# NSA and MoBA trunk on one core: chains of x by token tile and halves, the compression sum beside a query chunk, gate 1 summed in the first attention, half accumulators at the outputs

## The chip, the cores and the metric

The kernel runs on one core of a Trainium2 chip. The time is that of the whole execution on the device in microseconds. Three runs are timed; the profile is of one further execution.

## The reference

A trunk of two layers over x (256 tokens, width 1024). In each layer a normalised x is scaled and shifted by vectors made from c, goes through an attention mixer, and is added back times a gate. Layer 0 is an NSA mixer (16 query heads, 4 key heads of width 64; a compressed, a selected and a window branch, mixed by sigmoid gates; compression flattens 15 blocks of 32 tokens, stride 16, to 2048 and sends them through two matmuls), layer 1 a MoBA mixer (256 tokens are one block, so it is plain causal attention).

```python
cond = jax.nn.silu(c)
for i in range(DEPTH):
    shift, scale, gate = jnp.split(cond @ ada_w[i] + ada_b[i], 3, axis=-1)
    h = rms_norm(x, norm_g[i]) * (1 + scale[:, None, :]) + shift[:, None, :]
...
    x = x + gate[:, None, :] * y
...
q, kc, vc, ks, vs, kw, vw, gl, z = split_cols(h @ w_in, [Q_W] + [KV_W] * 6 + [3 * N_HEADS, Q_W])
...
    return jax.nn.gelu(flat @ cmp_w1[i] + cmp_b1[i]) @ cmp_w2[i]
...
    return gc[..., 0:1] * o_cmp + gc[..., 1:2] * o_slc + gc[..., 2:3] * o_win
...
return (o * jax.nn.silu(z)) @ w_out
```

## The kernel before

Every instruction is first recorded in a plan (class `Plan`) and then issued by its greedy list scheduler, so nearly every row of the profile has the line of that issue loop, L361, and rows are told apart by their tiles. Each recorded operation has a level: FIRST_OF_ALL (-2), URGENT (-1), CHAIN (0) or FILL (1); on each engine the ready operation with the lowest level goes first, by the planner's own cost estimates. Tiles come from tags with a few buffers each (`hi`, `lo`: 4, `raw`: 5, `early`: 12, `ps`: 6 and `acc`: 2 banks of PSUM); a `ps` bank is 512 columns.

Matmuls in full precision are made of three: each fp32 weight is split by `parts_of` into `hi` (cast by ScalarE) and `lo` (the rest, subtracted by VectorE), and `product` adds hi times hi, hi times lo and lo times hi. HT holds the transposed, normalised and scaled h in the same two parts; its scale and shift per column are the small tile AB.

In order of the work: (1) x is loaded, squared and scaled by its rstd (`rstd_of`, eight small VectorE steps from `ss` to `rs`), transposed into xT, and by `affine` and `h_parts` made into HT, one or two of its eight column tiles at a time, as the vectors shift and scale arrive. Those come from `ada_rows`: matmuls of `early` weights (1024 by 128 or 256) with condz, the silu of c, in four column groups of 32 rows (shift and scale, two groups each), a `row` copy, and the selP matmul that turns a row to columns. `SPINS` matmuls on the identity come before. (2) The k and v products, for each of four row groups kp and four column groups ci, in the order of the table START, with `ada_rows` between. (3) `make_k` norms and ropes the keys; the tables for rope and norm (`tables`, on GpSimd) come from positions and small vectors that SyncE loads in `small_loads`. FLAT holds the blocks for compression, p<-ps,RT in the rows. (4) `chunk` makes queries 0 to 255 and the branch gates in 304 columns, then the compression's first sum `hid` (acc<-raw,p in the rows), the gelu, then the next query chunk; with spread, `chunk` calls `beside` after each weight, which moves one step of the generators in the list `side`: gate 0, shift and scale of layer 1. (5) z by `z_blocks`, the first half at once, the second one step per pair. (6) Eight `pair_a` of the first attention, each with one `beside`. (7) `out_products` with 512-column accumulators per token tile m and half ch; after the last product of each, `x_half` updates X and squares it and `next_h` makes layer 1's HT. (8) Layer 1 likewise; gate 1 is summed by VectorE in `ada_gate(1)`, eight operations of 128 by 1024 spread over the query chunks, then a matmul with ones, and two additions onto a bias that a DMA has broadcast. (9) z, eight `pair_b`, the last `out_products`, and for each accumulator y = acc times gate, X + y, and the output's DMA.

## Time and profile before

| | us |
|---|---|
| median of three runs | 330.7 (329.78 to 332.0) |
| profiled execution | 330.94 |
| its span, first to last instruction | 329.2 |
| TensorE, VectorE, ScalarE busy | 314.0, 239.5, 196.0 |

The three runs are whole executions; the span leaves out 1.7 us before the first and after the last instruction. Busy time says how long an engine had an instruction in work; what counts for the time is where TensorE, which is busy 95% of the span, has nothing in work, and for whom it waits.

### The profile page before, as it was taken

How to read it: one execution, taken by the hardware profiler on the slowest of the kernel's cores; microseconds unless marked ns; L12 is line 12 of the kernel's file. 1: busy time of each engine (PE TensorE's matmuls, PEld its weight loads, DVE VectorE, ACT ScalarE, POOL GpSimd, SP SyncE). 2: the span in 40 equal slices, each digit the busy share in tenths (PEclk: the TensorE clock that was granted, in tenths of full speed). 3: DMA queues.
4: the chain of work that ended last, by engine and by line, in shares of the span. 5: the costliest groups of instructions: out<-in, count | busy, mean ns of one | idle time of the engine just before them, and what ended most of it. 6: DMA issues, size and time to landing. Idle time of an engine off the chain costs nothing.

```text
span 329.2 us, 5934 instructions
## 1 busy us (share of the span) xinstructions
PE 314.0 (95%) x2135; PEld 249.9 (76%) x2135; DVE 239.5 (73%) x569; ACT 196.0 (60%) x467; POOL 25.7 (8%) x97
## 2 busy tenths in 40 slices
PE   5899999999899999999999999989999989999994
PEld 4666676897668669867878878767777989888883
DVE  1643473789999869623788867699999999984663
ACT  4534153664796463553797973786467699884420
POOL 6000896000000000000000000000000000000000
PEclk9999999999999999999999999999999999999999
DMA  7989999545948698849337138237988450303002
GB/s 246 336 251 370 364 357 319 161 145 183 344 172 319 214 326 290 257 137 326 117 120 265 64 89 280 79 113 241 315 304 286 157 186 3 127 0 100 29 34 96
DMA packets 43876, 66.83 MB, mean 203 GB/s; under 512 B 3800, under 2 KB 20295, under 8 KB 43847
## 3 DMA queue, kind: packets, MB, share of 16 engines
q1 hardware_dynamic: 43678, 66.40, 60.7%
q8 instruction: 17, 0.28, 0.3%
q14 instruction: 13, 0.10, 0.1%
q10 hardware_dynamic: 168, 0.06, 0.1%
HBM read 65.40 MB, written 1.05 MB: 202 GB/s over the span
## 4 chain that ended last, share of the span: by engine, by line
PE 80%; DVE 8%; DMA 6%; ACT 3%; issue 1%; ACTq 0%; SPq 0%
PE ps L361 44%; PE acc L361 36%; DMA early<-in_nsa_w_in_dram 3%; DMA raw<-in_nsa_w_out_dram 2%; DMA y<-in_nsa_cmp_b_dram 2%; DVE rs L361 1%; ACT hi L361 1%; DVE n_out L361 1%; DVE lo L361 1%; DVE y L361 1%; DVE tiny L361 1%; ACT p L361 1%; DVE X L361 1%; DVE KTA L361 1%; ACTq L361 0%
## 5 line engine op out<-in xcount | busy, mean ns | idle before, releaser
L361 DVE TENSOR_TENSOR lo<-raw,hi 128x1024 fp32r<-128x1024 f32 (+1 forms) x50 | 59.2, 1186 | 12.6 <-ACT hi L361 12.1
L361 ACT CAST hi<-raw 128x1024 fp32r<-128x1024 f32 (+1 forms) x50 | 51.0, 1027 | 28.4 <-PE acc L361 11.6
L361 PE MATMUL acc<-hi,HT 128*128 128x512 f32 (+1 forms) x176 | 57.8, 392 | 0.1
L361 PE MATMUL acc<-HT,hi 128*128 128x256 f32 x256 | 49.0, 286 | 1.0 <-DVE zT L361 1.0
L361 ACT ACTIVATE p<-ps,tiny 128x128 f32<-128x128 f32 (+1 forms) x96 | 39.7, 436 | 4.8 <-DVE tiny L361 4.6
L361 PEld LDWEIGHTS acc<-HT,hi 128*128 128x128 f32 x256 | 40.0, 189 | 2.4 <-DVE zT L361 2.1
L361 PEld LDWEIGHTS acc<-hi,HT 128*128 128x128 f32 x176 | 32.2, 188 | 8.5 <-issue 1.1
L361 PE MATMUL acc<-HT,lo 128*128 128x256 f32 x128 | 36.5, 286 | 0.0
L361 PE MATMUL acc<-lo,HT 128*128 128x512 f32 (+1 forms) x88 | 34.0, 387 | 0.0
L361 PE MATMUL ps<-KTA,qg 128*128 128x256 f32 (+1 forms) x192 | 30.7, 297 | 0.0
L361 PE MATMUL ps<-hi,HT 128*128 128x512 f32 (+1 forms) x96 | 28.0, 364 | 0.0
L361 PEld LDWEIGHTS ps<-KTA,qg 128*128 128x128 f32 x192 | 26.2, 191 | 2.2 <-issue 1.5
L361 DVE TENSOR_REDUCE tiny<-ps 128x2 f32<-128x512 f32 (+2 forms) x40 | 24.8, 630 | 2.7 <-PE ps L361 2.4
L361 ACT COPY pT<-ps 128x384 f32<-128x384 f32 x48 | 21.2, 498 | 6.2 <-PE ps L361 6.2
L361 PEld LDWEIGHTS acc<-HT,lo 128*128 128x128 f32 x128 | 24.1, 189 | 0.3 <-issue 0.2
L361 PE MATMUL ps<-hi,qg 128*128 128x512 f32 x64 | 22.2, 395 | 0.0
L361 PE MATMUL acc<-hi,qg 128*128 128x512 f32 x64 | 22.0, 394 | 0.0
L361 ACT ACTIVATION_READ_ACCUMULATOR p<-ps,tiny 128x1 f32 x96 | 21.2, 221 | 0.0
L361 PE MATMUL ps<-identF,p 128*128 128x128 f32 x144 | 20.5, 275 | 0.4 <-ACT p L361 0.4
L361 PEld LDWEIGHTS ps<-hi,HT 128*128 128x128 f32 x96 | 17.1, 189 | 3.6 <-issue 1.2
L361 PEld LDWEIGHTS acc<-lo,HT 128*128 128x128 f32 x88 | 16.6, 188 | 3.3 <-issue 0.5
L361 PE MATMUL ps<-pT,VA 128*64 128x256 f32 (+1 forms) x192 | 18.7, 333 | 0.0
(194 smaller groups left out, 560.1 us busy)
## 6 DMA issues: line engine op xcount, KB each, us to landing
raw<-in_ada_w_dram SPq DMA_DIRECT2D x32, 512.0 KB, 4.3
raw<-in_moba_w_in_dram SPq DMA_DIRECT2D x20, 512.0 KB, 5.1
early<-in_ada_w_dram SPq DMA_DIRECT2D x16, 512.0 KB, 9.9
early<-in_nsa_w_in_dram SPq DMA_DIRECT2D x12, 512.0 KB, 8.7
raw<-in_nsa_w_in_dram SPq DMA_DIRECT2D x12, 512.0 KB, 4.3
raw<-in_nsa_cmp_w_dram SPq DMA_DIRECT2D x8, 512.0 KB, 4.4
raw<-in_nsa_w_out_dram SPq DMA_DIRECT2D x8, 512.0 KB, 3.7
raw<-in_moba_w_out_dram SPq DMA_DIRECT2D x8, 512.0 KB, 4.7
```

Source lines behind the costliest of these rows:

```text
L361: r = getattr(self.engines[e], method)(*[self._real(a) for a in args], **{k: self._real(a) for k, a in kw.items()})
```

## The change

- Start: the sum of squares, rstd and scaling are separate for the two token tiles, and the scaling goes by halves of 512 columns, half on VectorE and half on ScalarE. The transposed small vectors (`columns(R, 8)`) come behind them. The first two `ada_rows` (128 columns) are made in two halves of two column groups each, with the row copied by VectorE. AB is one operation less. `affine` writes HT's high part from ScalarE and VectorE makes the low part. The first weights are split by k. The small loads come one by one behind the weights of later kp, the tables after the eighth entry of START. The planner counts a DMA of short rows at 1.4 times its bytes. Spins use X, so they wait for its load.
- Compression's sum becomes `cmp_steps`, a generator in `side`, one step per weight of the first query chunk.
- Gate 0 and gate 1 take the bias as one row (of g, or of the gate tile, which GpSimd clears) instead of a broadcast to 128 rows and an addition; ScalarE copies the result. The eight operations of gate 1 all are multiply-adds, and stand in `side`, which `pair_a` moves on by three steps each (one for the last two).
- z's first half goes with `beside` steps; the second query chunk and MoBA's are without spread.
- `out_products` has two accumulators of 256 columns in place of the last 512 for token tile 0 in the first output and for tile 1 in the second; X's update, squares and output DMA go by these slices.

```diff
+    smalls = small_loads()
...
-                with plan.at(level), plan.group():
-                    for k in range(kk - run + 1, kk + 1):
-                        for s in range(2):
-                            j = s * 2 + k % 2
-                            T.matmul(acc[32 * j:32 * j + 32, :n], condz[:, k, :], w[s][:, k % step, :],
+                for half in ((0,), (1,)) if n == P else ((0, 1),):
+                    with plan.at(level), plan.group():
+                        for k in range(kk - run + 1, kk + 1):
+                            for s in half:
+                                j = s * 2 + k % 2
+                                T.matmul(acc[32 * j:32 * j + 32, :n], condz[:, k, :], w[s][:, k % step, :],
...
-        A.copy(g, acc[:, :n])
+        if n == P:
+            V.tensor_copy(g, acc[:, :n])
+        else:
+            A.copy(g, acc[:, :n])
...
-        Q.dma_start(gate, row_to_all(ada_b, l * 3 * D + 2 * D, D))
+        bias = bass.AP(tensor=ada_b.tensor, offset=ada_b.offset + l * 3 * D + 2 * D, ap=[[D, 1], [1, D]])
         if l:
-            acc = tile_of("gate", D)
+            G.memset(gate, 0.0)
+            Q.dma_start(gate[0:1], bias)
             for kk in range(8):
                 w = ada_piece(l, kk, 2 * D, D)[:, 0, :]
                 with plan.at(FILL):
-                    if kk:
-                        V.scalar_tensor_tensor(acc, w, condz[:, kk, 0:1], acc, op0=OP.mult, op1=OP.add)
-                    else:
-                        V.tensor_scalar_mul(acc, w, condz[:, kk, 0:1])
+                    V.scalar_tensor_tensor(gate, w, condz[:, kk, 0:1], gate, op0=OP.mult, op1=OP.add)
                 yield
...
-            V.tensor_add(gate[:, sl], t, gate[:, sl])
+                T.matmul(t, mix[s], src[s], start=True, stop=True)
+                A.copy(gate[:, s * 512:(s + 1) * 512], t)
...
-    columns(R, 8)
-    ss = tile_of("ss", 16)[:, 0:2]
+        ss = [tile_of("ss", 16)[:, 0:1] for m in range(2)]
...
-        r = rstd_of(ss, 2, 1.0 / D)
-        V.tensor_scalar_mul(xs[0], X[:, 0, :], r[:, 0:1])
-        A.activation(xs[1], X[:, 1, :], AF.Copy, scale=r[:, 1:2])
+        r = [rstd_of(ss[m], 1, 1.0 / D) for m in range(2)]
...
+    columns(R, 8)
...
-                    affine(hv[:, k, :], hv[:, k, :], 0, k0 + k, V)
-                h_parts(hv, k0, nk, 0, S)
+                    affine(HT[:, 0, k0 + k], hv[:, k, :], 0, k0 + k, A)
+                    h = tile_of("rot", S)
+                    affine(h, hv[:, k, :], 0, k0 + k, V)
+                    V.tensor_sub(HT[:, 1, k0 + k], h, HT[:, 0, k0 + k].bitcast(F32))
...
-    side += [ada_gate(0), ada_ss(1, 0, 4), ada_ss(1, 4, 4)]
+    side += [cmp_steps(hid), ada_gate(0), ada_ss(1, 0, 4), ada_gate(1), ada_ss(1, 4, 4)]
...
-    chunk(w_in, ((256, 256), (2560, 48)), q_and_gates)
+    chunk(w_in, ((256, 256), (2560, 48)), q_and_gates, spread=1)
...
-    chunk(w_in, ((512, 512),), raw_part(raw_q, 512), spread=1)
+    chunk(w_in, ((512, 512),), raw_part(raw_q, 512))
     make_q(raw_q, 0, QT, 2)
     zT = []
-    at_once(z_blocks(w_in, 2608, zT))
+    for _ in z_blocks(w_in, 2608, zT):
+        beside()
...
-        beside()
+        beside(3 if i < 6 else 1)
...
-        accs = [[tile_of("acc" if ch == 0 else "ps", 512) for m in range(2)] for ch in range(2)]
+        accs = {}
+        for ch in range(2):
+            for m in range(2):
+                halves = 2 if ch and m in fine else 1
+                n = 512 // halves
+                accs[m, ch] = [(slice(n * h, n * h + n), tile_of("ps" if ch else "acc", n)) for h in range(halves)]
...
-    side.append(ada_gate(1))
...
-    out_products(m_out, done_b)
+    out_products(m_out, done_b, (1,))
```

On TensorE at the first products, before: the end of the second visit (weights `early_4`, `early_5` with condz, alternating), then the first product of kp 0 (`acc`) and the selP matmul for the second row.

```order
L361 MATMUL ps_3_194<-early_4_212,condz_81 32x128
L361 MATMUL ps_3_194<-early_5_218,condz_81 32x128
L361 MATMUL ps_3_194<-early_4_212,condz_81 32x128
L361 MATMUL ps_3_194<-early_5_218,condz_81 32x128
L361 MATMUL acc_0_289<-hi_0_216,HT_125 128x512
L361 MATMUL acc_0_289<-lo_0_227,HT_125 128x512
L361 MATMUL acc_0_289<-hi_0_216,HT_125 128x512
L361 MATMUL ps_4_220<-selP_92,row_0_225 128x2
```

Now the visit is two blocks of eight, and they stand after the first product of weights ci 0 and inside that of ci 1:

```order
L364 MATMUL acc_0_267<-hi_0_250,HT_125 128x512
L364 MATMUL acc_1_270<-hi_0_250,HT_125 128x512
L364 MATMUL ps_5_222<-hi_1_272,HT_125 128x512
L364 MATMUL ps_0_153<-hi_1_272,HT_125 128x512
L364 MATMUL ps_4_203<-early_4_231,condz_81 32x128 x8
L364 MATMUL ps_5_222<-lo_1_280,HT_125 128x512
L364 MATMUL ps_5_222<-hi_1_272,HT_125 128x512
L364 MATMUL ps_0_153<-lo_1_280,HT_125 128x512
L364 MATMUL ps_0_153<-hi_1_272,HT_125 128x512
L364 MATMUL ps_4_203<-early_5_260,condz_81 32x128 x8
L364 MATMUL ps_3_195<-selP_92,row_0_248 128x2
```

The visit that stood before the first product now stands behind the first eight products and again behind four more, and the row that waits for it stands behind the second block.

On VectorE, before, the gate 1 sums (`gate_1<-raw,condz`) stand among MoBA's `lo` operations and rstd steps:

```order
L361 SCALAR_TENSOR_TENSOR gate_1_703<-raw_3_662,condz_81,gate_1_703 128x1024
L361 TENSOR_SCALAR rs_3_1100<-rs_3_1100 128x8
L361 TENSOR_TENSOR lo_2_299<-raw_1_634,hi_2_286 128x1024
L361 TENSOR_TENSOR rs_3_1100<-rs_3_1100 128x8
L361 SCALAR_TENSOR_TENSOR gate_1_703<-raw_2_646,condz_81,gate_1_703 128x1024
L361 TENSOR_TENSOR rs_3_1100<-rs_3_1100 128x8
L361 SCALAR_TENSOR_TENSOR rs_3_1100<-rs_3_1100 128x8
L361 TENSOR_TENSOR rs_3_1100<-rs_3_1100 128x8
L361 TENSOR_TENSOR lo_3_316<-raw_0_621,hi_3_297 128x1024
L361 TENSOR_TENSOR rs_3_1100<-rs_3_1100 128x8
L361 SCALAR_TENSOR_TENSOR gate_1_703<-raw_4_671,condz_81,gate_1_703 128x1024
```

Now they stand in the first attention, between softmax maxima (`tiny<-ps`), the normalisation of probabilities (`p<-p,tiny`) and the products with silu of z (`zT`):

```order
L364 TENSOR_REDUCE tiny_4_1216<-ps_0_153 128x2
L364 TENSOR_REDUCE tiny_4_1216<-ps_5_222 128x2
L364 SCALAR_TENSOR_TENSOR gate_0_164<-raw_4_704,condz_81,gate_0_164 128x1024
L364 SCALAR_TENSOR_TENSOR gate_0_164<-raw_0_629,condz_81,gate_0_164 128x1024
L364 TENSOR_REDUCE tiny_2_1184<-ps_0_153 128x4
L364 RECIPROCAL tiny_5_1224<-tiny_5_1224 128x8
L364 SCALAR_TENSOR_TENSOR tiny_5_1224<-tiny_5_1224,gates_136 128x4 x2
L364 TENSOR_TENSOR p_2_731<-p_2_731,tiny_5_1224 128x512
L364 TENSOR_SCALAR p_3_751<-p_3_751,tiny_5_1224 128x256 x2
L364 TENSOR_SCALAR p_4_1215<-p_4_1215,tiny_5_1224 128x256 x2
L364 TENSOR_REDUCE tiny_2_1184<-ps_5_222 128x2
L364 SCALAR_TENSOR_TENSOR zT_2_737<-y_0_145,acc_0_267 128x512
```

All eight moved from layer 1 to the first attention: two ahead of the first zT, six between the second and the third.

On VectorE at the end, before:

```order
L361 TENSOR_TENSOR X_69<-X_69,y_1_278 128x512
L361 TENSOR_TENSOR y_0_144<-acc_1_302,gate_0_395 128x512
L361 TENSOR_TENSOR X_69<-X_69,y_0_144 128x512
L361 TENSOR_TENSOR y_1_278<-ps_0_146,gate_0_395 128x512
L361 TENSOR_TENSOR X_69<-X_69,y_1_278 128x512
```

Now:

```order
L364 TENSOR_TENSOR y_1_373<-acc_0_267,gate_0_164 128x512
L364 TENSOR_TENSOR X_69<-X_69,y_1_373 128x512
L364 TENSOR_TENSOR y_0_145<-ps_5_222,gate_0_164 128x256
L364 TENSOR_TENSOR X_69<-X_69,y_0_145 128x256
L364 TENSOR_TENSOR y_1_373<-ps_4_203,gate_0_164 128x256
L364 TENSOR_TENSOR X_69<-X_69,y_1_373 128x256
```

The last 512 columns of token tile 1 are in two pieces of 256.

## Rows read from the trace of the kernel before

**Rows 1.** The page, part 1: busy time of each engine over the span.

```profile
PE 314.0 (95%) x2135; PEld 249.9 (76%) x2135; DVE 239.5 (73%) x569; ACT 196.0 (60%) x467; POOL 25.7 (8%) x97
```

**Rows 2.** Busy time by stages: window, then each engine's us (instructions), clock, DMA share, GB/s.

```profile
0.00:20.00 20.00, 13.95 (x109) 11.05 (x110) 8.60 (x29) 10.96 (x18) 5.17 (x32) 1.00 0.88 269
...
80.00:92.00 12.00, 10.42 (x90) 7.70 (x85) 11.24 (x31) 8.13 (x17) 0.00 (x0) 1.00 0.95 322
...
120.00:160.00 40.00, 40.00 (x337) 33.39 (x335) 22.31 (x45) 20.77 (x45) 0.00 (x0) 1.00 0.77 262
160.00:190.00 30.00, 29.58 (x238) 24.39 (x238) 26.47 (x74) 26.63 (x93) 0.00 (x0) 1.00 0.34 124
...
212.00:240.00 28.00, 26.48 (x116) 19.64 (x116) 25.55 (x47) 18.71 (x43) 0.00 (x0) 1.00 0.66 213
240.00:262.00 22.00, 22.00 (x132) 18.81 (x132) 21.80 (x46) 14.12 (x18) 0.00 (x0) 1.00 0.72 244
262.00:280.00 18.00, 16.97 (x155) 15.78 (x154) 17.51 (x49) 17.50 (x50) 0.00 (x0) 1.00 0.31 105
...
300.00:330.00 30.00, 24.64 (x119) 20.20 (x117) 16.75 (x24) 8.45 (x12) 0.00 (x0) 0.98 0.16 53
```

**Rows 3.** Timeline of TensorE at the start: start, us, instruction, [idle before <- releaser].

```profile
10.05 1.93 PE L361 MATMUL ps<-early,condz 128*32 128x128 f32 x30 [0.99 <-DMA early<-in_ada_w_dram]
...
16.37 1.07 PE L361 MATMUL ps<-early,condz 128*32 128x128 f32 x30 [0.63 <-DMA early<-in_ada_w_dram]
17.38 0.50 PE L361 MATMUL acc<-hi,HT 128*128 128x512 f32 x1
...
18.96 0.38 PE L361 MATMUL ps<-selP,row 128*128 128x2 f32 x2 [0.62 <-ACT row L361]
...
24.30 1.07 PE L361 MATMUL ps<-early,condz 128*32 128x256 f32 x16
25.30 0.50 PE L361 MATMUL acc<-hi,HT 128*128 128x512 f32 x1
```

**Rows 4.** Timeline of VectorE at the start, same columns.

```profile
8.53 0.26 DVE L361 COPY RT<-ps 128x100 f32<-128x100 f32 x1 [3.42 <-PE ps L361]
...
10.87 0.75 DVE L361 TENSOR_SCALAR n_in<-X,rs 128x1024 f32<-128x1024 f32 x1
```

**Rows 5.** Timeline of ScalarE at the start, same columns.

```profile
6.73 0.19 ACT L361 ACTIVATION_READ_ACCUMULATOR n_in<-X 128x1 f32 x1
```

**Rows 6.** Timeline of TensorE after 80 us: its idle times that are discussed.

```profile
83.16 0.66 PE L361 MATMUL ps<-identF,y 128*128 128x128 f32 x4 [1.24 <-ACT y L361]
...
88.53 1.57 PE L361 MATMUL ps<-identR,n_parts 128*128 128x128 f32 x16 [0.34 <-DVE n_parts L361]
...
221.54 1.40 PE L361 MATMUL ps<-identF,n_in 128*128 128x128 f32 x8 [0.98 <-DVE n_in L361]
...
271.21 0.38 PE L361 MATMUL acc<-HT,hi 128*128 128x256 f32 x1 [1.03 <-DVE zT L361]
```

**Rows 7.** Instructions grouped by shape: count | busy us, mean ns | idle before.

```profile
L361 DVE TENSOR_TENSOR lo<-raw,hi 128x1024 fp32r<-128x1024 f32 x46 | 56.0, 1220 | 12.1 <-ACT hi L361 11.6
...
L361 DVE SCALAR_TENSOR_TENSOR gate<-raw,condz,gate 128x1024 f32<-128x1024 f32 x7 | 9.0, 1280 | 0.0
...
L361 DVE TENSOR_TENSOR gate<-ps,gate 128x512 f32<-128x512 f32 x4 | 2.8, 688 | 1.7 <-PE ps L361 1.7
...
L361 ACT COPY row<-ps 128x512 f32<-128x512 f32 x3 | 1.8, 602 | 0.7 <-PE ps L361 0.7
...
L361 DVE TENSOR_TENSOR pc<-pc,tiny 128x256 f32<-128x256 f32 x4 | 1.7, 420 | 0.1
```

**Rows 8.** Timeline of TensorE and then VectorE at the end.

```profile
324.25 0.40 PE L361 MATMUL ps<-hi,qg 128*128 128x512 f32 x1
...
324.68 0.69 DVE L361 TENSOR_TENSOR y<-ps,gate 128x512 f32<-128x512 f32 x1 [1.33 <-PE ps L361]
325.40 0.69 DVE L361 TENSOR_TENSOR X<-X,y 128x512 f32<-128x512 f32 x1
```

More of the change, by code (lines that the diff above doesn't have):

```diff
@@ L611, in piece, with parts_of @@
         return t
-    def parts_of(t, into=None):
+    def parts_of(t, into=None, by_k=False):
         n = t.shape[2]
@@ L617, in parts_of @@
         with plan.at(FILL):
-            A.copy(hi, t)
-            V.tensor_sub(lo, t, hi.bitcast(F32))
+            for ks in (slice(k, k + 1) for k in range(KP)) if by_k else (slice(0, KP),):
+                A.copy(hi[:, ks], t[:, ks])
+                V.tensor_sub(lo[:, ks], t[:, ks], hi[:, ks].bitcast(F32))
         return hi, lo
@@ L1062, with cmp_steps @@
                                  pe[:, :, None, None].to_broadcast([64, 8, KVH, nu]))
-    side += [ada_gate(0), ada_ss(1, 0, 4), ada_ss(1, 4, 4)]
+    def cmp_steps(hid):
+        for kq in range(4):
+            w1 = [load(bass.AP(tensor=nsa_cmp_w1.tensor, offset=nsa_cmp_w1.offset + kv * 2048 * 256 + kq * 512 * 256,
+                               ap=[[256, P], [P * 256, 4], [1, 256]])) for kv in range(2)]
+            for k in range(4):
+                with plan.at(FILL), plan.group():
+                    for kv in range(2):
+                        T.matmul(hid[64 * kv:64 * kv + 64, 0:256],
+                                 FLAT[kv][kq // 2][:, 4 * (kq % 2) + k].rearrange("p g n -> p (g n)"), w1[kv][:, k, :],
+                                 start=(kq == 0 and k == 0), stop=(kq == 3 and k == 3), tile_position=(0, 64 * kv))
+            if kq < 3:
+                yield
+    hid = tile_of("ps", 512)
+    side += [cmp_steps(hid), ada_gate(0), ada_ss(1, 0, 4), ada_gate(1), ada_ss(1, 4, 4)]
     QT = qt_tiles()
@@ L1075, in q_and_gates @@
         V.tensor_scalar(gates[:, m, :, 2], gl[:, :, 1], 0.5, 0.5, op0=OP.mult, op1=OP.add)
-    chunk(w_in, ((256, 256), (2560, 48)), q_and_gates)
+    chunk(w_in, ((256, 256), (2560, 48)), q_and_gates, spread=1)
     make_q(raw_q, 0, QT, 0)
-    hid = tile_of("acc", 512)
-    for kq in range(4):
-        w1 = [load(bass.AP(tensor=nsa_cmp_w1.tensor, offset=nsa_cmp_w1.offset + kv * 2048 * 256 + kq * 512 * 256,
-                           ap=[[256, P], [P * 256, 4], [1, 256]])) for kv in range(2)]
-        for k in range(4):
-            with plan.at(FILL), plan.group():
-                for kv in range(2):
-                    T.matmul(hid[64 * kv:64 * kv + 64, 0:256],
-                             FLAT[kv][kq // 2][:, 4 * (kq % 2) + k].rearrange("p g n -> p (g n)"), w1[kv][:, k, :],
-                             start=(kq == 0 and k == 0), stop=(kq == 3 and k == 3), tile_position=(0, 64 * kv))
     hidS = tile_of("g", 256)
@@ L1311 @@
     raw_q = tile_of("n_in", 2, 512)
-    chunk(m_in, ((0, 512),), raw_part(raw_q, 512), spread=1)
-    beside(1)
+    chunk(m_in, ((0, 512),), raw_part(raw_q, 512))
     make_q(raw_q, 4, QT, 0)
     raw_q = tile_of("n_in", 2, 512)
-    chunk(m_in, ((512, 512),), raw_part(raw_q, 512), spread=1)
-    assert not side
+    chunk(m_in, ((512, 512),), raw_part(raw_q, 512))
     make_q(raw_q, 4, QT, 2)
```

94 lines of the change are left out of this document (57 added, 37 removed).

## The prediction

> **What bounds the kernel now.** I read the page's busy times first: TensorE is busy 314.0 of 329.2 us, VectorE 239.5, ScalarE 196.0 [rows 1]. Only the 15.2 us in which TensorE waits, and the work it is given, can change the time by much. Then I cut the span into stages [rows 2], to see where those 15 us lie: 6.05 before 20 us, 1.58 in 80 to 92, 0.42 in 160 to 190, 1.52 in 212 to 240, 1.03 in 262 to 280, and 5.36 in the last window, of which only the stretch up to the span's end at 329.2 counts (0.8 of it lies behind the end). Everywhere else TensorE has no hole. The reader is to see in the same rows that VectorE is nearly full just where TensorE waits (11.24 of 12 us in 80 to 92, 17.51 of 18 in 262 to 280), and that it has 17.7 us to spare in 120 to 160 but 3.5 in 160 to 190. Last I read the timelines around the holes [rows 3 to 6] and at the end [rows 8].
>
> The profiled execution took 330.94 us: 329.2 of span and 1.7 around it; the median of three runs is 330.7. The sum goes against 330.94; the 0.2 between the two is small beside every term's bounds and is left out. A run of this kernel can be told from another at about 1%, 3.3 us.
>
> **Part 1, the start.** The old chain to the first product at 17.38 is: both sums of squares ready on ScalarE at 6.92 [rows 5], rstd held behind the copy of RT at 8.53 because VectorE runs in order, scaling at 10.87 [rows 4], and the first shift and scale group at 10.05 after 0.99 us for a DMA [rows 3]. The change moves the RT copy behind the rstd steps, so scaled x is there about 1.5 us sooner (10.87 less 6.92 is 3.95, of which the rstd steps, from the copy's end at 8.79, are 2.1 and the copy's delay 1.9; two chains in place of one take some of it back). But the second chain, of shift and scale, starts with a DMA that nothing here makes earlier. Its tail gets shorter: the row copy no longer stands behind ScalarE's casts, AB has one operation less, and the affine writes HT directly. Between 15.5 and 17.0 for the first product I take 16.5, **-0.9**.
>
> What the split by halves costs: a whole visit of 32 instructions keeps four column groups busy, and 30 of them took 1.93 us at 10.05 and 1.07 us at 16.37 [rows 3]. The granted clock stands at 1.00, the full level of 2.4 GHz, in this window [rows 2], but the same work took 1.8 times as long in the first visit, as it would at 1.2 GHz. A half has 16 instructions on two of the column groups, so by the steps it makes it lasts as long as the whole: two halves cost 2 x 1.07. In the old order the second visit (16.37 to 17.38) lies before the first product, in time in which TensorE had nothing else. In the new order its two halves stand between products, on the path: 2 x 1.07 and about 0.25 for twice as many changes between the two shapes make **+2.4**. Against it go the idle times at the second visit's row and behind it (0.62 before selP at 18.96 and some 0.15), -0.8; and a new wait for a row that is now copied by VectorE between `lo` operations of 1.22 us [rows 7], +0.5 (at least 0, at most one such operation). Part 1: -0.9 + 2.4 - 0.8 + 0.5 = **+1.2**. If the halves fill waits that would be there anyway it is -0.5; if the first product comes no sooner than 17.0 and the row is late by a whole `lo`, +2.9.
>
> The Trainium skill, page "TensorEngine Tiling (Array Packing)", Key Properties, says that column tiles work independently and that a change of tiling mode drains the array. The rows bear out the cost of leaving the mode: a visit that is issued at 24.30 with 1.07 us is followed by a product at 25.30 [rows 3]. By the rule that tiles are independent, two halves could be free only if something else ran in the other two groups, and nothing does; with the rule alone one would put the cost at 1.07 plus the drains, and the sum would come out about 0.2 lower than with mine, since it prices no drain.
>
> **Part 2, compression beside the first query chunk (62 to 110).** The two holes of 1.24 and 0.34 us [rows 6] go (start to start they are worth 1.4 and 0.6, since the next load of weights is late too): -2.0. What is late next: the compression sum now stands ahead of the chunk's last products and needs the last of the additions that build its input, on VectorE; the gelu chain of short steps comes earlier and puts the next chunk's `lo` behind it; VectorE is 94% full there [rows 2]. I price three such waits at 0.6 (half a `lo`), 1.2 (a `lo` [rows 7]) and 1.0: +2.8. Sum **+0.8**, from -2.0 (all waits fall in other work) to +3 .
>
> **Part 3, first attention (120 to 190).** z's matmuls are now spread one step per pair, so TensorE has filler to the end of the stage; here I count the hole of 0.42 and the slow feeding around it, in all -1.0. The eight gate 1 sums move in: 8 x 1.28 = 10.2 us of VectorE [rows 7]. In 120 to 190 VectorE has 21.2 us free, but most of it before 160 [rows 2]; in the new order two of the sums stand ahead of the first zT and six between it and the third, among the later pairs. I take them as hidden: where they collide, softmax steps of the next pair slip, and TensorE has z and gate work to fill. Bounds: -3 and +6.7 (10.2 less the 3.5 free). Part 3: **-1.0**.
>
> **Part 4, the first output.** With 256-column accumulators for token tile 0, the last update of X in front of the next layer's norm is 2 x 0.42 instead of 2 x 0.69 [rows 7, 8], -0.5, less one extra addition. The hole of 0.98 at 221.54 is that of tile 1, which the halves do not touch. **-0.5** (from -1.0 to 0).
>
> **Part 5, MoBA's projections (212 to 280).** VectorE loses the 10.2 us of sums and four additions of 0.69 are now ScalarE copies of 0.60 [rows 7]; it was busy 64.9 of 68 us there [rows 2]. The holes of 0.98 (221.54) and 1.03 (271.21) [rows 6] both end with VectorE, so they should shrink. At 221.54 VectorE's own chain, not the sums, is long: half goes. At 271.21 all goes. With the smaller losses in 230 to 240: **-1.6** (from -2.6, every hole, to 0).
>
> **Part 6, the end.** After the last product (324.25 and 0.40) VectorE needs 0.69 + 0.69 before the last DMA is issued [rows 8]; with 256 columns 2 x 0.42, -0.55, and the DMA has half the bytes, -0.25 by estimate. 256-column matmuls cost a little more per column: +0.2. **-0.6** (from -0.8 to 0).
>
> The loads of small tables behind kv pieces, the tables on GpSimd (busy 5.17 us before 20 us, then none in any stage from 80 on [rows 2]) and a later planner cost for short rows I put at nothing: TensorE has no hole there, and the cover is the products' own time; if the tables came after the first rope, all of the rope's chain would be late, but their time is moved by less than the stage between.
>
> Sum: 1.2 + 0.8 - 1.0 - 0.5 - 1.6 - 0.6 = -1.7; 330.94 - 1.7 = **329.3 us**, no change by the bound of 1%.
>
> **Rivals.** *A, faster.* The start's halves hide in waits (-0.5), compression gives its 2.0 without new waits, attention -1.0, output -0.5, MoBA -1.6, end -0.6: -6.2, **324.7 us**. For it: each hole has an edit aimed at it, and TensorE is otherwise full, so a closed hole is time won. Against it: VectorE is full where the holes are, so it is likely that another wait on it comes last. Chance 0.30.
>
> *B, slower: VectorE in the first attention.* The sums fall between the softmax steps of 160 to 190, where it is busy 26.47 of 30 us. It decides if more than two of the eight run there beside the old work (2 x 1.28 is 2.6, the free time is 3.5, and each softmax step is waited for). With all of them there it costs 10.2 - 3.5 = 6.7, less what the other parts give (-1.7 + 1.0 = -0.7): up to 337; with five 2.9 + some queueing, I take +4.5, **334.7 us**. For it: six of the sums stand among the later pairs in the new order, and every pair's softmax waits for VectorE twice. Against it: z's work moves into the same stretch as filler, and MoBA gets the same 10.2 us back. Chance 0.17.
>
> *C, slower by the start.* TensorE keeps the slow pace into the products: each half then lasts 1.93 and not 1.07 [rows 3], 4 x 0.86 = 3.4 on top of the sum, **332.7 us**, within 1%. The trace speaks against it: the pace had risen before the visit at 16.37, and TensorE is fed as densely in the new order. Chance 0.08. The forecast itself has 0.45.
>
> **How the numbers follow.** Faster by over 1% (under 327.4): all of A but a little, and some of the forecast's own lower end: 0.34. Slower (over 334.0): two thirds of B and a little of C: 0.17. Within: 0.49. The range goes from 323.5, a little below A, to 334.5, B's lower part; what lies outside is A with part 3 at its bound, and B's worst. The forecast's own range, from the bounds that are likely together, is 327 to 332.
>
> **What would show it.** In the changed profile: first product between 15.5 and 17; two visits of some 1.1 us each between the first products; no hole with `y` as releaser after 80 us, but short ones with `lo` or `FLAT` work before 110; VectorE over 90% in 160 to 190 with TensorE still full; no hole on zT near 270; last VectorE operations of 0.42. I am wrong if holes on VectorE of more than 3 us in all show up between the pairs (B), or if no hole of over 0.3 us is left from 20 to 300 us (A).

## The result and the profile after

The changed kernel takes 333.17 us (median of ten runs, 331.47 to 334.84) against 330.0 (ten runs, 329.45 to 332.27) timed beside it: ratio 1.0079 (95% interval 1.005 to 1.0107), slower by 0.8%. The forecast was 329.3 us, 0.995 of the 330.94 from which the sum counts. "Within 1%" holds, and so does the range, but the time went up where it was to go down.

The profiled execution took 331.47 us, the shortest of the ten, with a span of 329.4. The unchanged program was profiled once more in the first experiment: 334.41 us, span 332.3. I read both, because the 2.9 us between them lie at nameable places.

Part 1 of the page, for [rows 1]:

```profile
PE 315.2 (96%) x2183; PEld 252.8 (77%) x2183; DVE 241.3 (73%) x581; ACT 199.9 (61%) x476; POOL 26.1 (8%) x98
```

Busy time by stages, with the edges and columns of [rows 2]:

```profile
0.00:20.00 20.00, 12.72 (x95) 9.98 (x96) 8.76 (x33) 10.90 (x17) 6.08 (x33) 1.00 0.99 305
...
80.00:92.00 12.00, 11.41 (x82) 7.58 (x81) 7.30 (x18) 7.51 (x17) 0.00 (x0) 1.00 0.92 303
...
120.00:160.00 40.00, 39.78 (x325) 31.73 (x326) 30.74 (x78) 28.32 (x86) 0.00 (x0) 1.00 0.61 211
160.00:190.00 30.00, 30.00 (x254) 23.16 (x251) 25.96 (x58) 21.77 (x78) 0.00 (x0) 1.00 0.64 212
...
262.00:280.00 18.00, 18.00 (x158) 16.23 (x158) 16.61 (x53) 16.02 (x51) 0.00 (x0) 1.00 0.27 90
```

Most holes did close: 11.41 of 12 us where it was 10.42, 30.00 of 30 where it was 29.58, 18.00 of 18 where it was 16.97. VectorE has more to spare in 80 to 92 (7.30 for 11.24) and no more to do in 160 to 190 (25.96 for 26.47); in 120 to 160 it has 30.74 for 22.31. The start has less (12.72 for 13.95). And TensorE is busy 1.2 us longer in all, with 48 more matmuls. A full window says nothing of how long the same work took, so I also compared the instants at which the two traces had done equal work: each matmul counts with a fixed time for its shape, and the sums are matched. This is worked out from all TensorE rows. The edge at 121 is uncertain by about 1 us, since z, gate 0 and shift and scale stand in another order there, and what one of its two neighbours gains by that the other loses. The last two rows are read directly: the first product of the last output starts at 302.43 before, and at 303.09 and 306.03 in the two profiles.

| stretch (us of before) | forecast | profile of 331.47 | profile of 334.41 |
|---|---|---|---|
| start, to 68 | +1.2 | +1.7 | +2.9 |
| to 121 (compression) | +0.8 | -0.8 | +0.3 |
| to 206 (first attention, output) | -1.0 - 0.5 | +1.5 | +2.2 |
| to 302 (MoBA, up to the last output) | -1.6 | -1.7 | -1.8 |
| sum before the last output | -1.1 | +0.7 | +3.6 |
| last output and end | -0.6 | -0.5 | -0.5 |

TensorE at the start, columns as in [rows 3]:

```profile
5.78 0.80 PE L364 MATMUL ps<-X,identF 128*128 128x128 f32 x2 [2.31 <-DMA X<-in_x_dram]
8.12 0.40 PE L364 MATMUL ps<-identF,y 100*128 100x100 f32 x1 [1.55 <-DMA y<-in_nsa_cmp_pe_dram]
8.31 1.53 PE L364 MATMUL ps<-X,identF 128*128 128x128 f32 x6
9.64 1.06 PE L364 MATMUL ps<-identF,n_in 128*128 128x128 f32 x4
10.63 1.51 PE L364 MATMUL ps<-early,condz 128*32 128x128 f32 x16
...
16.21 0.73 PE L364 MATMUL acc<-hi,HT 128*128 128x512 f32 x2 [0.20 <-ACT HT L364]
...
18.33 1.07 PE L364 MATMUL ps<-early,condz 128*32 128x128 f32 x16
...
20.45 1.07 PE L364 MATMUL ps<-early,condz 128*32 128x128 f32 x16
21.92 0.38 PE L364 MATMUL ps<-selP,row 128*128 128x2 f32 x2 [0.39 <-DVE row L364]
...
23.37 0.50 PE L364 MATMUL acc<-hi,HT 128*128 128x512 f32 x1 [0.50 <-ACT HT L364]
```

The first product comes at 16.21, 1.17 sooner than in [rows 3]. The two half visits of 1.07 stand between the products, as priced, and the row from VectorE is waited for by 0.39. That is about the copy's own time and not a wait behind `lo` work, for VectorE stood idle before it:

```profile
21.57 0.29 DVE L364 COPY row<-ps 128x128 f32<-128x128 f32 x1 [2.69 <-PE ps L364]
```

What I had not priced is the row at 8.31: six spins on X, behind a transpose that waits until 8.12 for a DMA, and ahead of the transposes of scaled x, which begin at 9.64.

In 80 to 110 TensorE has two new waits, on a buffer and on a `lo`, 0.82 together; the second profile has the same two (0.59 and 0.22, at 94.06 and 94.79):

```profile
91.66 0.49 PE L364 MATMUL acc<-hi,HT 128*128 128x512 f32 x1 [0.59 <-ACT n_in L364]
92.39 0.51 PE L364 MATMUL acc<-lo,HT 128*128 128x512 f32 x1 [0.23 <-DVE lo L364]
```

VectorE at the end, for [rows 8]; TensorE's last row starts at 325.48 there, before at 324.25:

```profile
325.79 0.42 DVE L364 TENSOR_TENSOR y<-ps,gate 128x256 f32<-128x256 f32 x1 [0.54 <-PE ps L364]
326.25 0.42 DVE L364 TENSOR_TENSOR X<-X,y 128x256 f32<-128x256 f32 x1
```

From TensorE's last start to the end of the span it is 329.4 - 325.48 = 3.9 us; before it was 329.2 - 324.25 = 4.95. Against these 1.0 us the products of the last output take longer: from the first start to the last 22.39, where it was 21.82.

### The profile page after: what moved, and what is told of

Read it like the earlier page. It is cut to its first block, busy times and chain, and to the rows that moved or that the text cites. A ratio compares the mean times of both kernels' runs of the same rounds, so it can differ in the third digit from the quotient of the medians.

```text
span 329.4 us, 6082 instructions
## 1 busy us (share of the span) xinstructions
PE 315.2 (96%) x2183; PEld 252.8 (77%) x2183; DVE 241.3 (73%) x581; ACT 199.9 (61%) x476; POOL 26.1 (8%) x98
## 4 chain that ended last, share of the span: by engine, by line
PE 89%; DVE 3%; ACT 2%; issue 0%; ACTq 0%
PE ps L364 51%; PE acc L364 38%; DVE lo L364 1%; ACT HT L364 1%; DVE rs L364 1%; ACT n_out L364 0%; ACT n_in L364 0%; ACT hi L364 0%; DVE g L364 0%; DVE HT L364 0%; DVE y L364 0%; DVE pcT L364 0%; DVE X L364 0%; ACT pcT L364 0%; DVE n_in L364 0%
## 5 line engine op out<-in xcount | busy, mean ns | idle before, releaser
L364 PE MATMUL acc<-hi,HT 128*128 128x512 f32 (+1 forms) x176 | 54.1, 382 | 1.3 <-ACT HT L364 0.7
L364 PE MATMUL acc<-HT,hi 128*128 128x256 f32 x256 | 54.3, 297 | 0.0
L364 PEld LDWEIGHTS acc<-HT,hi 128*128 128x128 f32 x256 | 40.9, 189 | 1.4 <-issue 0.9
L364 PE MATMUL ps<-hi,HT 128*128 128x512 f32 (+1 forms) x96 | 28.7, 365 | 0.0
L364 PE MATMUL ps<-hi,qg 128*128 128x256 f32 (+1 forms) x96 | 23.7, 321 | 0.0
L364 PE MATMUL ps<-identF,p 128*128 128x128 f32 x144 | 21.5, 275 | 0.0
L364 PEld LDWEIGHTS acc<-lo,HT 128*128 128x128 f32 x88 | 16.5, 188 | 5.0 <-DVE lo L364 1.1
```

The source lines that it names most:

```text
L364: r = getattr(self.engines[e], method)(*[self._real(a) for a in args], **{k: self._real(a) for k, a in kw.items()})
```

## The experiments

Ratios are to the kernel before (medians of 330.0 to 330.9, taken beside each group of runs) with 95% intervals; experiments 9 to 12 ran on another chip than the rest. Experiments 1 to 4 ran side by side, so their medians compare directly; later ones are set against the changed kernel's two ratios, 1.0079 and 1.0097, and a difference then has two ends. Letters of theories are those of the quoted texts.

**1. The changed kernel again**, with no edit.

> The changed kernel once more, for a second profile beside the first, whose execution (331.47 us) was the shortest of ten around a median of 333.2. Ratio to the kernel before 1.008 again. Theory P (the pace of TensorE at the start differs between executions, since its first work now waits for x): this profile, if it is a longer one, loses the difference of 1 to 3 us before the first 20 us are over, with a first product at 17 to 18.5 instead of 16.2 or slow products behind it, and equal distances from there on. Theory S (something later differs, a transfer or a wait on VectorE): the first 20 us are equal within 0.3 us and the difference comes in a later stage.

Measured: 333.75 us, 1.0097 (1.0076 to 1.0117). TensorE's start, and 82 us, in its profile:

```profile
8.94 0.40 PE L364 MATMUL ps<-identF,y 100*128 100x100 f32 x1 [2.62 <-DMA y<-in_nsa_cmp_pe_dram]
...
11.45 1.92 PE L364 MATMUL ps<-early,condz 128*32 128x128 f32 x16
...
17.43 0.74 PE L364 MATMUL acc<-hi,HT 128*128 128x512 f32 x2 [0.21 <-ACT HT L364]
...
82.18 0.65 PE L364 MATMUL ps<-raw,p 128*64 128x256 f32 x2 [0.26 <-DMA raw<-in_nsa_cmp_w_dram]
83.54 1.94 PE L364 MATMUL ps<-raw,p 128*64 128x256 f32 x14 [0.72 <-DMA raw<-in_nsa_cmp_w_dram]
```

The small table of the compression landed 0.82 us later (8.94 for 8.12), the first visit took 1.92 for 1.51, and both together move the first product by 1.22. At 82 us the compression sum waits for its own weights, 0.26 and 0.72: a new wait, which the shorter execution does not show as idle. Theory P holds for 1.2 of the 2.9 us; its equal distances behind the start do not, since these waits add as much again. So the loss at the start is real and varies, and so does the result of part 2.

**2. Visits whole again**, row on ScalarE.

```diff
-                for half in ((0,), (1,)) if n == P else ((0, 1),):
+                for half in ((0, 1),):
...
-        if n == P:
-            V.tensor_copy(g, acc[:, :n])
-        else:
-            A.copy(g, acc[:, :n])
+        A.copy(g, acc[:, :n])
```

> The changed kernel with each 128-column visit of shift and scale in one piece of four column groups and the row copied by ScalarE, as before. Theory H (halves between the products cost some 2 us of TensorE's time): 1.5 to 2.5 us shorter than the changed kernel, ratio to the kernel before 1.000 to 1.003. Rival (the halves stand in waits that are there anyway, and the loss lies in the first attention): no change, ratio 1.006 to 1.010.

Measured: 332.01 us, 1.0044 (1.003 to 1.0058), 1.7 us better than experiment 1. The second visit of its profile, on TensorE:

```profile
20.53 1.08 PE L364 MATMUL ps<-early,condz 128*32 128x128 f32 x32
22.08 0.38 PE L364 MATMUL ps<-selP,row 128*128 128x2 f32 x2 [0.47 <-ACT row L364]
```

32 matmuls on four column groups take 1.08, and 16 on two take 1.07: the split buys nothing per visit and costs the second one, as the prediction priced it. The gain is that of theory H (1.5 to 2.5), the ratio a little above its 1.003.

**3. Spins on the identity** in place of X.

```diff
-            T.matmul(spin[:, 0:P], identF, X[:, 1, 0:P], start=True, stop=True)
+            T.matmul(spin[:, 0:P], identF, identF, start=True, stop=True)
```

> The changed kernel with the spins on the identity again, so that TensorE has work from 1.4 us on and not only when x is loaded. Theory P (late and varying pace): the median falls by 1.5 us or more and the runs lie closer together, ratio 1.000 to 1.004. Rival (the pace at the start is hidden behind the chain of shift and scale): within 0.5 us of the changed kernel, ratio 1.006 to 1.010.

Measured: 331.78 us, 1.0038 (1.002 to 1.0055), 2.0 better than experiment 1. Its TensorE rows show the queue without the six spins:

```profile
4.63 1.06 PE L364 MATMUL ps<-identF 128*128 128x128 f32 x4
8.44 0.28 PE L364 MATMUL ps<-identF,y 100*128 100x100 f32 x1 [2.74 <-DMA y<-in_nsa_cmp_pe_dram]
8.57 0.63 PE L364 MATMUL ps<-identF,n_in 128*128 128x128 f32 x4
```

The transposes of scaled x come right behind that of the table, at 8.57. The two waits of the changed kernel at 21.92 (row) and 23.37 (HT), 0.89 together, have no counterpart over 0.2 in this profile. The gain is that of theory P, but its reason, a varying pace, is not shown: the runs lie no closer together (330.63 to 332.73). The edit of one word in the spins is worth as much as the split.

**4. Gate 1 in layer 1 again.**

```diff
-    side += [cmp_steps(hid), ada_gate(0), ada_ss(1, 0, 4), ada_gate(1), ada_ss(1, 4, 4)]
+    side += [cmp_steps(hid), ada_gate(0), ada_ss(1, 0, 4), ada_ss(1, 4, 4)]
...
-        beside(3 if i < 6 else 1)
+        beside()
...
+    side.append(ada_gate(1))
...
-    chunk(m_in, ((0, 512),), raw_part(raw_q, 512))
+    chunk(m_in, ((0, 512),), raw_part(raw_q, 512), spread=1)
+    beside(1)
...
-    chunk(m_in, ((512, 512),), raw_part(raw_q, 512))
+    chunk(m_in, ((512, 512),), raw_part(raw_q, 512), spread=1)
+    assert not side
```

> The changed kernel with gate 1 summed among layer 1's projections again (one step of the side work per pair, spread over the two query chunks). Theory G (the sums in the first attention cost more there than they free later): 1 to 3 us shorter than the changed kernel, ratio 0.999 to 1.005. Rival (they are hidden there, and layer 1 gains 2.4 us by their absence, as the two profiles show between 212 and 280 us): 1.5 to 2.5 us longer than the changed kernel, ratio 1.012 to 1.016.

Measured: 333.61 us, 1.0089 (1.0062 to 1.0116): no change, outside both theories. By equal work the first attention wins 1 to 2 us and layer 1 loses about 2.5, where the hole on zT is back (1.01 at 274.30). The sums' place is a wash within the noise: what MoBA gained by their absence the attention lost.

**5. Accumulators of 512 at both outputs.**

```diff
-    FINE = (0,)
+    FINE = ()
...
-    out_products(m_out, done_b, (1,))
+    out_products(m_out, done_b, ())
```

> The changed kernel with 512-column accumulators at both outputs, as before. Theory F (the halves at the outputs give what was forecast, 0.5 and 0.6 us): 0.7 to 1.5 us longer than the changed kernel, ratio 1.011 to 1.014. Rival (what the shorter tail gives, the extra matmuls and the later first output take back): within 0.5 us, ratio 1.007 to 1.010.

Measured: 335.17 us, 1.0122 (1.0096 to 1.0147), so the halves are worth 0.8 to 1.4 us (0.0025 and 0.0043 of 330.9); the smaller of the two is not clear of the noise. The prediction's parts 4 and 6 had 0.5 and 0.6.

**6. The compression sum behind the chunk again.**

```diff
-    hid = tile_of("ps", 512)
-    side += [cmp_steps(hid), ada_gate(0), ada_ss(1, 0, 4), ada_gate(1), ada_ss(1, 4, 4)]
+    side += [ada_gate(0), ada_ss(1, 0, 4), ada_gate(1), ada_ss(1, 4, 4)]
...
-    chunk(w_in, ((256, 256), (2560, 48)), q_and_gates, spread=1)
+    chunk(w_in, ((256, 256), (2560, 48)), q_and_gates)
     make_q(raw_q, 0, QT, 0)
+    hid = tile_of("acc", 512)
+    at_once(cmp_steps(hid))
...
-    chunk(w_in, ((512, 512),), raw_part(raw_q, 512))
+    chunk(w_in, ((512, 512),), raw_part(raw_q, 512), spread=1)
```

> The changed kernel with the compression's first sum behind the first query chunk again, and the side work spread over the second chunk. Theory C (the sum beside the chunk now waits for its weights, 1.0 us of waits for a DMA at 82 to 84 us in the longer of the two profiles, and costs more than the two holes that it closed): 0.5 to 1.5 us shorter than the changed kernel, and no wait of TensorE on the compression's weights. Rival (closing the holes gives the 1 to 2 us that the first profile shows between 62 and 120): 1 to 2 us longer, with holes of over 1 us near 80 to 92 again.

Measured: 336.7 us, 1.0172 (1.0151 to 1.0194). The waits of its TensorE (total us, times, longest) have the old one back, and more on VectorE:

```profile
PE acc L364 <- DVE lo L364: 1.4, 3, 0.7
PE ps L364 <- ACT y L364: 1.2, 1, 1.2
```

In this surrounding the move is worth 2.5 to 3.1 us (0.0075 and 0.0093 of 330.9), where I had counted a cost of 0.8: the rival's direction, and more than its 1 to 2.

**7 and 8. Both undone at the start**: the edits of 2 and 3 together; then also 13 spins for 8.

> The changed kernel with both: spins on the identity and whole visits. Theory: the two costs lie one behind the other at the start (spins on x stand 1.5 us in TensorE's queue ahead of the transposes of scaled x; halves take 2 us between products), so they add: 3 to 4 us shorter than the changed kernel, ratio 0.998 to 1.001. Rival (both wait for the same thing, the shift and scale of the first column tile): no more than the better of them alone, ratio 1.003 to 1.005.

> As the kernel before it, with 13 spins in place of 8, so that TensorE also has work from 5.7 to 8.4 us, where it stood still. Theory P (the pace of the first transposes and visits is set by what TensorE did before): transposes of scaled x at 0.11 instead of 0.22 us each from the first on, first product 0.5 to 1.5 us sooner, 0.5 to 1.5 us shorter than with 8 spins. Rival (the first product waits for ScalarE and the shift and scale rows): pace higher or not, first product and time within 0.4 us of those with 8 spins.

Measured: 331.3 us, 1.0009 (0.9989 to 1.0028), and 330.19 us, 0.9977 (0.9961 to 0.9993). The first takes back nearly the whole loss, 2.3 to 2.9 us; the second is the best version found and is 0.2% shorter than the kernel before. The two costs do not add in full (1.7 and 2.0 alone). For 13 spins theory P has the time right, about 1 us, but its mechanism is not shown: in this profile, of its longest execution (331.73), the transposes of scaled x still take 0.22 each and the first product comes at 18.00, where with 8 spins it came at 16.16. Experiment 9 has the same start and shows 0.13 for eight of them and 16.70, so this start too varies between executions. On TensorE:

```profile
16.05 0.35 PE L364 MATMUL ps<-selP,row 128*128 128x2 f32 x2 [1.91 <-ACT row L364]
18.00 0.51 PE L364 MATMUL acc<-hi,HT 128*128 128x512 f32 x1 [1.59 <-ACT HT L364]
...
18.66 1.93 PE L364 MATMUL ps<-early,condz 128*32 128x128 f32 x32
```

and its windows there:

```profile
18.00:20.00 2.00, 2.00 (x30) 1.51 (x34) 1.46 (x2) 0.92 (x1) 0.00 (x0) 0.66 1.09 349
20.00:22.00 2.00, 2.00 (x16) 1.33 (x9) 0.18 (x1) 0.78 (x2) 0.00 (x0) 0.50 1.09 348
```

Behind rests of 1.91 and 1.59 us the granted clock was 0.66 and then 0.50, the lower level of 1.2 GHz, and the whole visit took 1.93. The start has room even in the best version.

**9, 13 and 14. z in groups of six matmuls**: on top of 8, of the changed kernel, and of the kernel before.

```diff
-                for b in range(4):
-                    cols = slice(b * P, (b + 1) * P)
-                    with plan.at(FILL):
-                        for i, (a, part) in enumerate(((0, 0), (0, 1), (1, 0))):
+                for h in range(2):
+                    with plan.at(FILL), plan.group():
+                        for b in (2 * h, 2 * h + 1):
+                            cols = slice(b * P, (b + 1) * P)
+                            for i, (a, part) in enumerate(((0, 0), (0, 1), (1, 0))):
```

The reason is TensorE's row of the first attention in the changed kernel:

```profile
139.23 1.02 PE L364 MATMUL ps<-row,selG 128*128 128x512 f32 x2
139.69 0.68 PE L364 MATMUL acc<-HT,hi 128*128 128x256 f32 x1
140.21 0.28 PE L364 MATMUL acc<-HT,lo 128*128 128x256 f32 x1
140.33 0.28 PE L364 MATMUL acc<-HT,hi 128*128 128x256 f32 x1
140.45 0.49 PE L364 MATMUL ps<-identF,p 128*128 128x128 f32 x3
140.69 0.36 PE L364 MATMUL acc<-HT,hi 128*128 128x256 f32 x1
140.89 0.28 PE L364 MATMUL acc<-HT,lo 128*128 128x256 f32 x1
```

From one z matmul to the next it is 0.12 us (140.21 to 140.33), but 0.20 for the first behind transposes (140.69 to 140.89) and 0.52 behind the gate's sum (139.69 to 140.21). Of 157 steps from one z matmul to the next 29 take more than 0.15; before it was 10 of 178, since z lay in longer runs. The distances of all 192 to the next start add up to 27.36 us (24.70 before), and no row shows them as idle. Not all of it is lost, since the other rows of the attention take less in return, such as pcT,Vbd 2.73 for 3.68 and pc,pc 0.56 for 0.92. Counted over z and all the attention's other rows, without idle time and without gate 1's matmuls, it is 88.6 us for 86.9, so 1.8 us are lost.

> The kernel with 13 spins and whole visits, with z's matmuls issued in groups of six (two column blocks, three products each) where they were issued one by one between the matmuls of the pairs. In the changed kernel's profile the first z matmul behind a transpose or a score takes 0.20 to 0.52 us to the next and the others 0.117, and there are 29 such entries in the first attention where before had 10. Theory I (filler in small pieces costs TensorE's own time): fewer entries (37 in place of 52 over both layers), 1 to 2 us shorter than with single issue, ratio 0.992 to 0.995. Rival (finer filler hides waits that the groups would show): equal or up to 1 us longer, ratio 0.997 to 1.001.

> The changed kernel with nothing but z's matmuls in groups of six. Theory I (single z matmuls between fp32 matmuls cost TensorE some 0.09 to 0.4 us at each entry): z's 192 matmuls of the first attention take 25 us from start to start as in before, not 27.4 to 27.9; 1 to 2.5 us shorter than the changed kernel, ratio 1.001 to 1.006, unless the weights of the first output land late, which stands there as a wait on a DMA near 190 us. Rival (groups show waits that single matmuls had filled): ratio 1.008 to 1.012 with holes of TensorE between the pairs.

> The kernel before with z's matmuls in groups of six. It has 23 entries over both layers in its order, of which 10 in the first attention cost more than 0.15 us; 17 with groups. Theory I: little to win, ratio 0.996 to 1.000. Rival (the order's other shifts decide): outside of that on either side.

Measured: 329.93 us, 0.9991 (0.9968 to 1.0013); 333.51 us, 1.0079 (1.006 to 1.0099); 331.74 us, 1.0038 (1.0025 to 1.0052). The grouped 192 take 24.97, 24.88 and 23.33 us, 2.3 to 2.5 less in the changed kernels, but their neighbours take 1.2 more (row,selG 1.32 for 0.92, pcT,Vbd 3.00 for 2.73), so about 1.0 us of TensorE's time is won. The time does not fall: 9 and 13 have the ratios of the rivals, and the kernel before is slower by 0.4%, with a hole on zT of 1.60 where it had 1.03. Experiment 9 shows where it went. On TensorE at the first output:

```profile
191.14 1.05 PE L364 MATMUL ps<-selP,row 128*128 128x2 f32 x8 [0.70 <-ACT row L364]
...
193.35 0.50 PE L364 MATMUL acc<-lo,qg 128*128 128x512 f32 x1 [0.52 <-DVE lo L364]
...
195.79 0.39 PE L364 MATMUL ps<-lo,qg 128*128 128x256 f32 x1 [0.52 <-DVE lo L364]
```

On ScalarE there:

```profile
193.43 1.05 ACT L364 CAST hi<-raw 128x1024 fp32r<-128x1024 f32 x1 [1.40 <-DMA raw<-in_nsa_w_out_dram]
```

TensorE gets to the first output sooner, with no other work left, and meets weights that are not ready: it waits 0.52 for the first `lo`, and 0.52 for the next, whose cast on ScalarE waited 1.40 for the weights' DMA. In the changed kernel ScalarE's casts wait there too (0.89 and 0.72 at 192.90 and 195.15), but TensorE still has the last pairs' work. Experiment 13 has the same waits as 9 at the row and the first `lo` (0.70 and 0.53). By equal work the two lose 2.5 and 1.9 us between 190 and 206, the changed kernel 0.2. This is the rival of experiment 9, finer filler that hides waits.

**10 and 12. The start of before with the rest of the change**; 12 with z in groups as well. The start's edits (scaling chains, halves, affine, loads, the planner's 1.4, spins) are taken out of the changed kernel.

> The changed kernel with the whole start of before (spins, one rstd chain for both tiles, the small vectors transposed first, whole visits, AB, affine and low parts, the small loads at once, the tables earlier); all of the change behind the start stays. Theory: the start costs the 1.7 to 2.6 us that the two profiles of the changed kernel show at equal work near 25 to 60 us, or more where DMAs land later; 2 to 3.5 us shorter than the changed kernel, ratio 0.998 to 1.003. Rival (what is lost at the start is made up by waits further on): within 1 us of the changed kernel.

> The start of before, all else of the change, and z's matmuls in groups of six (24 entries over both layers in place of 54). Theory I: 1.5 to 3 us shorter than with the start of before alone, ratio 0.990 to 0.996. Rival: equal to it within 0.7 us.

Measured: 333.99 us, 1.0103 (1.0066 to 1.0139), and 341.28 us, 1.0327 (1.0296 to 1.0358). Neither is the sum of its parts. Experiment 10 is within 1 us of the changed kernel, as its rival had it: without the new start nothing is won in the time. By equal work it stands 0.5 ahead of before at 60 us, where the changed kernel is 1.7 to 2.9 behind, and then loses about 3.5 between 84 and 97, the changed kernel 1.0. On TensorE:

```profile
89.40 0.49 PE L362 MATMUL acc<-hi,HT 128*128 128x512 f32 x1 [0.58 <-ACT n_in L362]
90.13 0.49 PE L362 MATMUL acc<-lo,HT 128*128 128x512 f32 x1 [0.23 <-DVE lo L362]
...
92.22 0.69 PE L362 MATMUL ps<-pc,pc 128*128 128x64 f32 x2 [0.61 <-DVE pc L362]
92.66 0.77 PE L362 MATMUL acc<-hi,HT 128*128 128x512 f32 x1
93.23 0.63 PE L362 MATMUL acc<-lo,HT 128*128 128x512 f32 x1
93.66 0.63 PE L362 MATMUL acc<-hi,HT 128*128 128x512 f32 x1
```

Its window there:

```profile
92.00:95.00 3.00, 2.78 (x9) 2.36 (x10) 3.00 (x13) 1.66 (x3) 0.00 (x0) 0.52 0.97 348
```

The granted clock is 0.52, the lower level, behind three short rests, and the products start 0.43 to 0.57 apart, where 0.23 is usual. In 12 the same stretch costs the same, and by equal work about 7 more us go between 160 and 190. TensorE, ScalarE and VectorE there:

```profile
172.12 0.38 PE L362 MATMUL acc<-HT,hi 128*128 128x256 f32 x1 [2.40 <-ACT hi L362]
174.39 0.38 PE L362 MATMUL acc<-HT,lo 128*128 128x256 f32 x1 [1.88 <-DVE lo L362]
...
171.03 1.04 ACT L362 CAST hi<-raw 128x1024 fp32r<-128x1024 f32 x1 [6.93 <-DMA raw<-in_nsa_w_in_dram]
...
167.96 5.24 DVE L362 SCALAR_TENSOR_TENSOR gate<-raw,condz,gate 128x1024 f32<-128x1024 f32 x4
```

z's weights come late, ScalarE's cast waits 6.93 for them, and the `lo` then stands behind four sums of gate 1 that VectorE works off in one piece (to 173.20). This is the collision of rival B, in a run where z lies in groups and the sums in the attention. Behind these rests the granted clock was 0.61 from 174 to 178, and the transposes behind them wait three times about 0.6 for pT.

**11. Compression and gate 1 both undone**, on top of 8. **15. Gate 1 in layer 1**, on top of 9.

> The kernel with 13 spins and whole visits (0.9977), with the compression behind the first query chunk and gate 1 in layer 1 again, both undone together. Undone alone in the changed kernel the compression cost 2.8 us and gate 1 nothing. Theory A (the parts add): 0.9977 plus 0.0085, ratio 1.004 to 1.008. Rival O (the undone compression alone pushed its neighbours' side work into a first attention that was already loaded by gate 1's sums; with both undone this is gone): ratio 0.996 to 1.001.

> Spins 13, whole visits, z in groups (0.9991) and gate 1 summed in layer 1 as before. Theory D (in the grouped kernel the weights of gate 1 keep the five raw buffers so long that the first output's weights land late, which cost a hole of 1.7 us at 190 to 196 us): the hole goes, and what layer 1 loses by the sums is 1 to 2 us: ratio 0.996 to 1.000. Rival G (the sums themselves in the first attention are what costs): ratio under 0.995.

Measured: 337.58 us, 1.022 (1.0188 to 1.0252), and 331.98 us, 1.0053 (1.0031 to 1.0074). The first is worse than either theory had it. Waits on `lo` of 2.2 us and on ScalarE's y of 1.7 come back; but most of the loss, over 7 us by equal work in the profile of its longest execution (340.21), lies between 121 and 160, with rests of 0.70 and 0.89 and a granted clock of 0.69 from 136 to 140 behind them. The second is outside both theories: the hole at the first output is gone, as D had it, but layer 1 loses about 1.5 against before, where experiment 9 gained.

**16. The start alone** on the kernel before (its gate biases as rows too, which the code shares).

> The new start alone: compression, z, gate 1 and the outputs as before (gate 0 and gate 1 keep the bias as a row). Theory: the start costs 1.7 to 2.9 us at equal work by 60 us, and nothing behind it gives that back: ratio 1.005 to 1.010. Rival (the holes at 80 to 92 us absorb it, since they wait for other engines): ratio 0.999 to 1.003.

Measured: 334.8 us, 1.0135 (1.0112 to 1.0158), +4.4 us: more than the whole change, and outside both theories. By equal work 2.1 of it are there by 60 to 76 us; the rest is lost behind 76, up to 215 us, with waits such as 0.77 (80.19), 0.56 (123.17) and 0.66 (218.99).

## Why the prediction was wrong

**Parts 3 and 4, first attention and output, are the step that failed most.** The forecast was -1.0 and -0.5, the traces show +1.5 and +2.2 for both together, a miss of 3.0 and 3.7 us, where the whole sum missed by 1.9 and 4.8. "I take them as hidden" and "TensorE has filler to the end of the stage" counted only idle time, and TensorE was indeed full, 30.00 of 30. What failed is the price of the filler, which the sum put at nothing: with 29 slow steps of z for 10, the same matmuls of z and the attention take 1.8 us more, all of it busy time. Rival B's condition was met, for five of the eight sums stand between 161 and 177, but the holes that it promised did not come. Experiment 4 shows that the sums do cost the attention 1 to 2 us, as layer 1 gains by their absence; experiment 12 shows the collision itself. How they cost it in the changed kernel, where TensorE has no hole, is not shown. Experiments 9 and 13 show that the price of z cannot be taken out alone: TensorE then stands at the output, whose weights are not ready.

**Part 1, the start, had the right sign, but its size was too small.** Forecast +1.2. The traces show +1.7 and +2.9 by 68 us, and in the start alone 2.1 by 76 (experiment 16, 4.4 in its whole time). Taking the split and the spins back won 1.7 and 2.0 us, both together 2.3 to 2.9; experiment 10, which takes back the whole start, won nothing, so that this loss alone does not explain the time. Of its terms "2 x 1.07" for the halves held, and 16.5 for the first product in one profile (16.21) and not in the other (17.43). The -0.8 for idle times at the row and behind it failed: 0.39 and 0.50 are there in place of 0.62 and 0.15. The +0.5 came near that 0.39 by luck, for no `lo` was in the way. Missing was a term for "Spins use X": the spins on X stand in TensorE's queue behind the transpose of a table whose DMA lands at 8.1 to 8.9 us, and put 1.3 us of filler ahead of the transposes of scaled x. The first half of scaled x is ready at 8.1 and its transposes begin only at 9.64. I had written "TensorE is fed as densely in the new order". The 0.25 for changes of shape has no row behind it: the first half takes 0.99 us from its start to that of the next product (18.33 to 19.32), and the product at 25.30 in [rows 3] starts before the modelled end of the visit at 24.30, so that row does not show the drain that I read in it. Nor does "about 0.2 lower" follow: with one visit's 1.07 the sum would be lower by up to 1.3. The Trainium skill, page "TensorEngine Tiling (Array Packing)", Key Properties, says that tiles operate independently. The rows agree: 16 matmuls on two groups take 1.07 and 32 on four 1.08, so a half costs as much as the whole.

**Part 2, compression, cost less than forecast.** Forecast +0.8, by traces -0.8 and +0.3; experiment 6 has the move worth 2.5 to 3.1 in the surrounding of the changed kernel. The holes on y and n_parts went, as said. "I price three such waits at 0.6, 1.2 and 1.0" was too much: VectorE was less full in 80 to 92 (7.30 of 12) after the move, and the new waits were 0.82 at 92 us and, in one profile, 0.98 for the compression's own weights.

**Part 5 held**: -1.7 and -1.8 for -1.6, and the hole on zT is gone. But the hole before tile 1's norm, half of which was to go, stayed (1.01 at 225.67). Of the "four additions" only two stood in this stage.

**Part 6 held in its sum**, -0.5 for -0.6, not in its terms: the end behind the last product is 1.0 shorter for 0.8, and the 256-column products cost 0.57 for 0.2. No row stands behind its 0.25 for the DMA; from VectorE's last operation to the end of the span it was 3.1 us before and is 2.7 now. Parts 4 and 6 together had 1.1, experiment 5 has 0.8 to 1.4.

**Rival C** came near in its number, 332.7, by luck: the first half visit at 1.51 and 1.92 is a slow pace at the start (granted clock 1.00 in its windows), but the halves between the products took 1.07, where C had 1.93.

Neither sign of being wrong came, holes on VectorE between the pairs or no hole left at all. Both looked at idle time, and the attention's loss is busy time.

What stays open: the later losses of experiments 10 and 16, and why 11 and 12 lose so much more than their parts. These orders are the list scheduler's, and they differ everywhere; the runs show where the time goes and the waits there, but not one edit that causes them.

## What to carry to other kernels

Filler on an in-order queue is only free if its own operand is early: follow what stands ahead of it and behind it, not only what it fills. When a hole closes on an engine that is 95% busy, look for the next late thing (here the compression's weights, then the output's) before you book the gain, and compare the time at equal work, since a full window hides slower work. Parts of a scheduled order don't add: measure them alone and undone, and run the kernel twice before you explain 1%.

## What the runs showed that I had not expected

- One program, two executions, 331.47 and 334.41 us: a small DMA that lands at 8.12 or 8.94 and a first visit of 1.51 or 1.92 make 1.2 us, and a wait for weights the same again.
- z's matmuls behind other work take 0.20 (behind transposes) or 0.52 us (behind the gate's sum of 512 columns) to the next start, where 0.12 is usual; nothing of it shows as idle time. But a third to a half of the sum came back as shorter rows beside it (1.1 of 2.9 from before to the changed kernel, 1.2 of 2.2 by grouping), so such a price is read over a matmul and its neighbours together.
- In experiment 10 three rests of 0.58, 0.23 and 0.61 us within 3 us were followed by a granted clock of 0.52 for the next 3 us, in a stretch that ran at 1.00 before; in the changed kernel rests of 0.59 and 0.23 at the same place were not (1.00 from 92 to 95).
